# A two-block model on one core: the overflow branch behind expert 60, row-tiled sums for experts 60 to 63, and the last down matrix in another cut

## The chip, the core and the metric

The kernel runs on one core of a Trainium2 chip. The core's engines work side by side, each on its own queue of instructions: TensorE (PE) multiplies matrices, VectorE (DVE), ScalarE (ACT) and GpSimd (POOL) work on elements, and SyncE (SP) issues nearly all transfers. Sixteen DMA engines carry the transfers. The metric is the device time of one execution in microseconds (us); less is better.

## The reference, cut to what matters

The model maps 256 tokens of width 1024 through a short convolution block, an attention block, and a second block that ends in a mixture of 64 experts. Only the end of the second block is touched:

```python
def hier_moe(x, ...):            # 256 tokens; each goes to 2 of 64 experts
    ...
    def run_block(args):
        xb, e = args
        h = jax.nn.silu(xb @ w_gate[e]) * (xb @ w_up[e])   # 1024 -> 512
        return h @ w_down[e]                               # 512 -> 1024
    ...
    y = jnp.zeros((N, D)).at[slot_tok].add(ys * slot_gate[:, None])

h = h + hier_moe(rms_norm_2(h, norm2_gain), ...)
return rms_norm_2(h, final_gain)                           # the output
```

All matrices are in float32. One expert's gate, up and down matrix are 2 MB each, so the 64 experts are 384 MB that must come in from memory.

## The kernel before

Up to about 700 us of the span the kernel computes the first block and the mixer. From then on it goes through the experts in order, `for e in range(64)` (L1964). The experts are in groups of four (`q = e // 4`, `i = e % 4`). Each expert has room for 32 tokens (`CAP`), so a group fills the 128 columns or rows of TensorE.

**One expert.** `gateup(e)` (L1897) multiplies the gathered tokens with gate and up: eight steps of contraction, and in each of them four products that stand in four groups of 32 columns of TensorE and run at once. ACT and DVE form silu(gate) times up. `hidden(e)` (L1915) transposes the result on TensorE and copies it (DVE). `down(e)` (L1925) multiplies with the down matrix: four steps of contraction (`j`), and in each four products of 256 columns (`m`), again in four column groups at once. Four ACT copies (L1940) put the 32 rows of this expert into its place of `st["Y", q]`. At the end of a group `combine(q)` (L1942) multiplies the four experts' rows with the gates of the group, `st["C", q]` (made by `dtrans(q)`, L1880: one POOL product, two transposes, one ACT copy), and adds them up in four PSUM banks, `self.acc`, over all groups.

**Loads.** `moe_load` (L1654) issues the matrices from SP in the order of `ORDER` (number m = 3 e + 0, 1 or 2 for gate, up and down; at the end 189, 190, 188, 191, which is gate 63, up 63, down 62, down 63). SP reuses eight semaphores in turn, and before it issues a load it waits until the load of the same semaphore has landed: eight loads are under way at any time. `done(m)` (L1957) says how far the loads may be issued; SP is some four experts ahead of TensorE. Every matrix but the last is cut by rows, so that each of the 128 partitions reads one piece of 8 or 16 KB. The last one (m = 191, L1664 to L1669) is cut by columns: two loads of 512 columns, four pieces of 2 KB for each partition.

**The branch.** `overflow()` (L1809) handles tokens beyond the 32 of an expert. With these inputs it isn't taken. All engines read the count (L1812), compare and jump over it (L1813). On SP the other arm of this `If` waits on each of the eight load semaphores in turn and adds to it what the loads of the skipped body would have added. The branch stands behind expert 52 (`OVERFLOW_AFTER`), where SP has issued the loads up to m = 168, gate 56; at expert 60 `done(182)` has let out all 192.

**The end.** `self.busy(n)` (L311) is n products of 128 columns whose result nobody reads. They stand ahead of expert 62 (`WARM1` = 8) and in the last two experts (`WARM2`). For expert 63 `last(hf)` (L2001) multiplies with one half of the columns, and `total(hf)` (L2015) sums that half for group 15, squares it (ACT, with the sum of squares) and, for the left half, multiplies with the final gain (DVE). So the left half is summed, squared and scaled before the right half is multiplied. Then the norm (DVE, POOL), the scaling with it (ACT for the left halves, DVE for the right ones) and four transfers out (L2041) end the program.

Of the kernel before, what the change touches and what calls it, by code (L numbers as in the profile page):

```python
# [176 lines left out]
WARM, WARM1, WARM2, WARM4 = 12, 8, (14, 5, 0, 3), 11  # L177
# [19 lines left out]
OVERFLOW_AFTER = 52  # L197


class Build:  # L200
# [1453 lines left out]
    def moe_load(self, n):  # L1654

        a = self.a
        while self.npart < min(n, 192):
# [4 lines left out]
            if g == 2 and e == 63:  # L1664
                w = a["w_down_2"][0, e].rearrange("(k p) n -> p k n", p=128)
                self.wt[m] = []
                for j, t in enumerate(places):
                    t = t.rearrange("p (k n) -> p k n", k=4)
                    self.dma_in_order(t, w[:, :, 512 * j:512 * j + 512])  # L1669
                    self.wt[m].append(t)  # L1670
                continue
# [26 lines left out]
    def moe(self, out):  # L1698
# [191 lines left out]

        def cols(w, j, e):

            if e == 63:
                return w[:, 256 * j:256 * j + 256]
            return w.rearrange("q (p j k) -> q j p k", j=2, k=2)[:, j]
# [19 lines left out]
        def hidden(e, tile="rb3"):  # L1915

            b = self.bank()
            for k in range(2):
                x = st["h", e][:, k:k + 255:2] if e < 63 else st["h", e][:, 128 * k:128 * k + 128]
# [5 lines left out]
        def down(e, hT=None):  # L1925
            q, i = divmod(e, 4)
            hT = hT or hidden(e)
            b2 = self.bank()
            for j in range(4):
                for m in range(4):  # L1930
                    mm(b2[32 * m:32 * m + 32, :256], lhsT=hT[j], rhs=self.wt[3 * e + 2][j][:, m * 256:m * 256 + 256],  # L1931
                       start=j == 0, stop=j == 3, skip_group_check=True, tile_position=(0, 32 * m))
# [9 lines left out]
        def combine(q, ms=range(4)):  # L1942
            for m in ms:
                for tt in range(2):
                    i = mm(self.acc[2 * tt + m // 2][:, (m % 2) * 256:(m % 2) * 256 + 256],  # L1945
                           lhsT=st["C", q][:, tt * 128:tt * 128 + 128], rhs=st["Y", q][m],
                           start=False, stop=q == 15, skip_group_check=True)
                    if q == 15:
                        self.tc.keep_in_program_order(i)
# [14 lines left out]
        for e in range(64):  # L1964
            q, i = divmod(e, 4)
            if e == 62:
                self.busy(WARM1)
# [15 lines left out]
            if i == 3 and q < 15:  # L1983
                combine(q)
                dtrans(q + 1)


        hT = hidden(62)
        if OVERFLOW_AFTER == 62:
            overflow()  # L1990
        self.busy(WARM2[0])
        gateup(63)
        hT2 = hidden(63, "rb")
        self.busy(WARM2[1])
        down(62, hT)
        hT = hT2
        self.busy(WARM2[2])
        fs = sm("fs", 4)
        fs = fs.rearrange("p (t c) -> p t c", t=2)

        def last(hf):  # L2001
            b2 = self.bank()
            for j in range(4):
                for m in (2 * hf, 2 * hf + 1):
                    i = mm(b2[32 * m:32 * m + 32, :256], lhsT=hT[j], rhs=self.wt[191][hf][:, j, m % 2 * 256:m % 2 * 256 + 256],  # L2005
                           start=j == 0, stop=j == 3, skip_group_check=True, tile_position=(0, 32 * m))
                    self.tc.keep_in_program_order(i)
            for m in (2 * hf, 2 * hf + 1):
                o = st["Y", 15][m][96:128]
                if m % 2 == 0:  # L2010
                    A.activation(o, b2[32 * m:32 * m + 32, :256], AF.Copy)  # L2011
                else:
                    V.tensor_copy(o, b2[32 * m:32 * m + 32, :256])

        def total(hf):  # L2015
            combine(15, (2 * hf, 2 * hf + 1))
            for tt in range(2):
                scr = self.xp.tile([128, 512], BF16, name="yl", bufs=2)
                A.activation(scr, self.acc[2 * tt + hf], AF.Square, accum_out=fs[:, tt, hf:hf + 1])  # L2019
                if hf == 0:  # L2020
                    V.tensor_tensor(out=xt[tt][:, :512], in0=self.acc[2 * tt], in1=fg[:, :512], op=ALU.mult)

# [79 lines left out]
```

## Time and profile before

| | us |
|---|---|
| median of 3 runs | 1665.9 (1664.17 to 1668.14) |
| the profiled execution: its own time | 1667.51 |
| the profiled execution: span from first to last instruction | 1665.7 |
| of the span: TensorE busy | 1354.8 (81%) |
| DVE, ACT, POOL busy | 581.4, 498.4, 85.7 |
| bytes moved by DMA | 520.92 MB, mean 313 GB/s |

The times of a row are counted from the first instruction of the span. A busy TensorE is not one at its peak, since matmuls overlap; a float32 product shows as two instructions. Where two engines are busy together, only the one that the next step waits for counts, so the profile is read stage by stage, and from the end back.

### The profile page before, as it was taken

What the parts mean: (1) busy time and instruction counts of PE and PEld (TensorE: products, weight loads), DVE (VectorE), ACT (ScalarE), POOL (GpSimd) and SP (SyncE); (2) the same over time, 40 slices, a digit from 0 to 9 for tenths busy, and PEclk for the clock granted to TensorE, in tenths of its full rate; (3) what the DMA queues carried; (4) which work ended last, traced back from release to release, by engine and by line L of the source; (5) the groups of instructions that cost most, each with busy time, mean ns of one, the idle gap of its engine ahead of it and who ended that gap; (6) DMA issues with size and microseconds to landing.
All of it is one profiled execution on the core that took longest, in us unless ns stands there. A gap on an engine that the chain in (4) does not pass through costs nothing. (4 is left out here: it accounts for less than half of the span.)

```text
span 1665.7 us, 29509 instructions
## 1 busy us (share of the span) xinstructions
PE 1354.8 (81%) x12874; PEld 1063.8 (64%) x12874; DVE 581.4 (35%) x1043; ACT 498.4 (30%) x940; POOL 85.7 (5%) x121
## 2 busy tenths in 40 slices
PE   8999999999999989998867766666765776766666
PEld 8999999999999988885534433433433443333334
DVE  5777565877655567751100000000000000000001
ACT  4454444646444455631111110111111111111112
POOL 2000000210000051120000000000000000000000
PEclk9999999999999999999989889888888889888889
DMA  8555545443645544399999999999999999998996
GB/s 286 203 182 190 191 159 185 152 151 120 209 153 200 178 144 148 129 381 409 426 428 428 425 428 429 426 427 429 426 427 430 426 427 428 427 426 344 425 429 277
DMA packets 130917, 520.92 MB, mean 313 GB/s; under 512 B 6816, under 2 KB 84128, under 8 KB 96864
## 3 DMA queue, kind: packets, MB, share of 16 engines
q1 hardware_dynamic: 130496, 518.46, 78.0%
q8 instruction: 103, 1.69, 0.4%
q10 hardware_dynamic: 288, 0.52, 0.1%
q14 instruction: 30, 0.25, 0.0%
HBM read 517.91 MB, written 1.05 MB: 312 GB/s over the span
## 5 line engine op out<-in xcount | busy, mean ns | idle before, releaser
L1906 PE MATMUL bank<-gu,x 128*32 128x256 f32 x2400 | 265.4, 468 | 149.6 <-DMA gu<-in_w_up 97.8
L265 DVE TENSOR_TENSOR wl<-slot,wh 128x1024 fp32r<-128x1024 f32 (+1 forms) x210 | 256.3, 1222 | 125.7 <-ACT wh L264 124.8
L264 ACT ACTIVATE wh<-slot 128x1024 fp32r<-128x1024 f32 (+1 forms) x213 | 223.4, 1052 | 231.5 <-PE bank L274 149.6
L1906 PEld LDWEIGHTS bank<-gu,x 128*32 128x32 f32 x2400 | 114.8, 129 | 259.8 <-DMA gu<-in_w_up 111.8
L1912 DVE TENSOR_TENSOR dg<-dg,bank 64x256 f32<-64x256 f32 x64 | 27.1, 423 | 687.0 <-ACT dg L1911 687.0
L274 PE MATMUL bank<-x,wh 128*128 128x256 f32 x864 | 245.1, 284 | 0.0
L273 PE MATMUL bank<-x,wh 128*128 128x256 f32 x864 | 244.7, 283 | 0.0
L275 PE MATMUL bank<-x,wl 128*128 128x256 f32 x864 | 244.6, 283 | 0.0
L1906 PE MATMUL bank<-slot,x 128*32 128x256 f32 x1456 | 175.9, 446 | 36.3 <-DMA slot<-in_w_up 30.5
L1911 ACT ACTIVATE dg<-bank 64x256 f32<-64x256 f32 x64 | 24.0, 375 | 499.1 <-PE bank L1906 499.1
L1940 ACT ACTIVATE x<-bank 32x256 f32<-32x256 f32 x252 | 94.3, 374 | 240.2 <-PE bank L1931 234.1
L275 PEld LDWEIGHTS bank<-x,wl 128*128 128x128 f32 x864 | 165.9, 192 | 0.0
L274 PEld LDWEIGHTS bank<-x,wh 128*128 128x128 f32 x864 | 165.8, 192 | 0.0
L273 PEld LDWEIGHTS bank<-x,wh 128*128 128x128 f32 x864 | 165.8, 192 | 0.0
L274 PE MATMUL acc<-yl,wh 128*128 128x256 f32 x480 | 136.3, 285 | 0.0
L275 PE MATMUL acc<-yh,wl 128*128 128x256 f32 x480 | 136.1, 285 | 0.0
L273 PE MATMUL acc<-yh,wh 128*128 128x256 f32 x480 | 135.0, 285 | 1.2 <-ACT yh L349 1.2
L1906 PEld LDWEIGHTS bank<-slot,x 128*32 128x32 f32 x1456 | 74.4, 122 | 89.9 <-DMA slot<-in_w_up 42.8
L1931 PE MATMUL bank<-gu,rb 128*32 128x256 f32 x1248 | 77.5, 389 | 22.5 <-DVE rb L1922 11.3
L273 PEld LDWEIGHTS acc<-yh,wh 128*128 128x128 f32 x480 | 91.1, 192 | 1.9 <-ACT yh L349 1.8
L274 PEld LDWEIGHTS acc<-yl,wh 128*128 128x128 f32 x480 | 92.1, 192 | 0.2
L275 PEld LDWEIGHTS acc<-yh,wl 128*128 128x128 f32 x480 | 92.1, 192 | 0.1
(408 smaller groups left out, 1799.2 us busy)
## 6 DMA issues: line engine op xcount, KB each, us to landing
gu<-in_w_down SPq DMA_DIRECT2D x39, 2048.0 KB, 26.8
gu<-in_w_gate SPq DMA_DIRECT2D x39, 2048.0 KB, 27.4
gu<-in_w_up SPq DMA_DIRECT2D x35, 2048.0 KB, 26.8
slot<-in_w_up SPq DMA_DIRECT2D x47, 1024.0 KB, 24.6
slot<-in_w_gate SPq DMA_DIRECT2D x44, 1024.0 KB, 25.1
slot<-in_w_down SPq DMA_DIRECT2D x42, 1024.0 KB, 27.0
slot<-in_conv_ffn_w SPq DMA_DIRECT2D x33, 1024.0 KB, 5.0
slot<-in_mla_ffn_w SPq DMA_DIRECT2D x33, 1024.0 KB, 5.0
```

The lines of the kernel that those rows point to most:

```text
L264: i = nc.scalar.activation(h, src, AF.Copy)
L265: j = (low or nc.vector).tensor_tensor(out=l, in0=src, in1=h.bitcast(F32), op=ALU.subtract)
L273: mm(out, lhsT=wh, rhs=xh, start=start, stop=False, skip_group_check=skip)
L274: mm(out, lhsT=wh, rhs=xl, start=False, stop=False, skip_group_check=skip)
L275: mm(out, lhsT=wl, rhs=xh, start=False, stop=stop, skip_group_check=skip)
L1906: mm(b[32 * j:32 * j + 32, 0:256], lhsT=X[k][:, 32 * i:32 * i + 32], rhs=cols(self.wt[3 * e + j // 2][k], j % 2, e), start=k == 0, stop=k ...
L1911: A.activation(s[64:128], b[0:64, 0:256], AF.Silu)
L1912: V.tensor_tensor(out=s[0:64], in0=s[64:128], in1=b[64:128, 0:256], op=ALU.mult)
L1931: mm(b2[32 * m:32 * m + 32, :256], lhsT=hT[j], rhs=self.wt[3 * e + 2][j][:, m * 256:m * 256 + 256], start=j == 0, stop=j == 3, skip_group_ ...
L1940: A.activation(o, s, AF.Copy)
```

## The change

- `OVERFLOW_AFTER` goes from 52 to 60. The branch itself stays as it is.
- The last down matrix is cut by rows as well, but in another order of rows than the others. Row 32 j + 4 i + k of the matrix goes to partition 16 i + j; the loads hold k = 0, 1 and k = 2, 3. So each partition reads one piece of 8 KB in each of the two loads, and the outermost dimension of the source, i, has 8 rows. The columns of gate and up of expert 63 are taken in the same order (`cols`), and `hidden(63)` needs no case of its own.
- Experts 60 to 63 have no common `combine(15)`. Their down products (`product`) have 512 columns: column groups 0 and 1 hold the two halves of the result, groups 2 and 3 hold them once more. One ACT copy takes all 128 rows over (`sums`), and four products, one in each row group of 32 rows (`tile_position=(32 * m, 0)`), add token half m // 2 and column half m % 2 into bank m.
- `dtrans_last` makes the gates for this: for each of the four experts the gate columns four times over (4 POOL products, 8 transposes, 4 ACT copies, behind `combine(14)`).
- All `busy` products from expert 62 on are gone.
- The end is: hidden of 62, gate and up of 63, hidden of 63, then the products of 62, the first half of the contraction of 63, the sums of 62, the second half of 63, and the sums of 63. All four banks are squared after that; three of the four quarters are multiplied with the gain by DVE and scaled by ACT, and the fourth is done by DVE in one operation.

```diff
--- before.py
+++ after.py
@@ -174,7 +174,7 @@
 
 
 RING = 7
-WARM, WARM1, WARM2, WARM4 = 12, 8, (14, 5, 0, 3), 11
+WARM, WARM4 = 12, 11
 
 
 
@@ -194,7 +194,7 @@
 
 LOW_CONV, LOW_MLA, LOW_MIXER = (2,), (("dkv", 192),), ("gg2",)
 CAP = 32
-OVERFLOW_AFTER = 52
+OVERFLOW_AFTER = 60
 
 
 class Build:
@@ -1654,7 +1654,6 @@
     def moe_load(self, n):
 
 
-
         a = self.a
         while self.npart < min(n, 192):
             m = ORDER[self.npart]
@@ -1662,12 +1661,12 @@
             e, g = divmod(m, 3)
             places, both = self.moe_places(m)
             if g == 2 and e == 63:
-                w = a["w_down_2"][0, e].rearrange("(k p) n -> p k n", p=128)
+
+                w = a["w_down_2"][0, e].rearrange("(j i k) n -> i j k n", i=8, k=4)
                 self.wt[m] = []
                 for j, t in enumerate(places):
-                    t = t.rearrange("p (k n) -> p k n", k=4)
-                    self.dma_in_order(t, w[:, :, 512 * j:512 * j + 512])
-                    self.wt[m].append(t)
+                    self.dma_in_order(t, w[:, :, 2 * j:2 * j + 2].rearrange("i j k n -> i j (k n)"))
+                    self.wt[m] += [t[:, 1024 * k:1024 * k + 1024] for k in range(2)]
                 continue
             k = 4 if g == 2 else 8
             w = a[("w_gate_2", "w_up_2", "w_down_2")[g]][0, e].rearrange("(p k) n -> p k n", k=k)
@@ -1888,10 +1887,25 @@
             A.activation(ct, b[:, :256], AF.Copy)
             st["C", q] = ct
 
+        def dtrans_last():
+
+            for i in range(4):
+                Dq = self.xp.tile([128, 2, 128], F32, name="yl", bufs=2)
+                GP.tensor_tensor(out=Dq.rearrange("p t (r c) -> p t r c", r=4),
+                                 in0=st["G", 15][:, :, i:i + 1, :].to_broadcast([128, 2, 4, 32]),
+                                 in1=gt[:, :, 60 + i:61 + i, None].to_broadcast([128, 2, 4, 32]), op=ALU.mult)
+                b = self.bank()
+                for tt in range(2):
+                    PE.transpose(b[:, tt * 128:tt * 128 + 128], Dq[:, tt], I)
+                if i % 2 == 0:
+                    ct = self.xtile(6 + i // 2)
+                A.activation(ct[i % 2], b[:, :256], AF.Copy)
+                st["C", 15, i] = ct[i % 2]
+
         def cols(w, j, e):
 
             if e == 63:
-                return w[:, 256 * j:256 * j + 256]
+                return w.rearrange("q (c i j k) -> q j i c k", i=8, j=2, k=2)[:, j]
             return w.rearrange("q (p j k) -> q j p k", j=2, k=2)[:, j]
 
         def gateup(e, ks=range(8)):
@@ -1916,20 +1930,31 @@
 
             b = self.bank()
             for k in range(2):
-                x = st["h", e][:, k:k + 255:2] if e < 63 else st["h", e][:, 128 * k:128 * k + 128]
+                x = st["h", e][:, k:k + 255:2]
                 PE.transpose(b[:, 64 * k:64 * k + 64], x, I[0:64, 0:64])
             hT = self.rp.tile([128, 256], F32, name=tile)[:, :128]
             V.tensor_copy(hT, b[:, 0:128])
             return [hT[:, 64 * (j % 2) + 32 * (j // 2):64 * (j % 2) + 32 * (j // 2) + 32] for j in range(4)]
 
-        def down(e, hT=None):
+        def product(e, hT, b2, js=range(4)):
+
+
+            w = 512 if e >= 60 else 256
+            for j in js:
+                for m in range(4):
+                    c = m % 2 if e >= 60 else m
+                    i = mm(b2[32 * m:32 * m + 32, :w], lhsT=hT[j], rhs=self.wt[3 * e + 2][j][:, c * w:c * w + w],
+                           start=j == 0, stop=j == 3, skip_group_check=True, tile_position=(0, 32 * m))
+                    if e >= 62:
+                        self.tc.keep_in_program_order(i)
+
+        def down(e):
             q, i = divmod(e, 4)
-            hT = hT or hidden(e)
+            hT = hidden(e)
             b2 = self.bank()
-            for j in range(4):
-                for m in range(4):
-                    mm(b2[32 * m:32 * m + 32, :256], lhsT=hT[j], rhs=self.wt[3 * e + 2][j][:, m * 256:m * 256 + 256],
-                       start=j == 0, stop=j == 3, skip_group_check=True, tile_position=(0, 32 * m))
+            product(e, hT, b2)
+            if q == 15:
+                return sums(e, b2)
             if i == 0:
                 st["Y", q] = []
                 for m in range(2):
@@ -1939,14 +1964,24 @@
                 o, s = Y[m][32 * i:32 * i + 32], b2[32 * m:32 * m + 32, :256]
                 A.activation(o, s, AF.Copy)
 
-        def combine(q, ms=range(4)):
-            for m in ms:
+        def combine(q):
+            for m in range(4):
                 for tt in range(2):
-                    i = mm(self.acc[2 * tt + m // 2][:, (m % 2) * 256:(m % 2) * 256 + 256],
-                           lhsT=st["C", q][:, tt * 128:tt * 128 + 128], rhs=st["Y", q][m],
-                           start=False, stop=q == 15, skip_group_check=True)
-                    if q == 15:
-                        self.tc.keep_in_program_order(i)
+                    mm(self.acc[2 * tt + m // 2][:, (m % 2) * 256:(m % 2) * 256 + 256],
+                       lhsT=st["C", q][:, tt * 128:tt * 128 + 128], rhs=st["Y", q][m],
+                       start=False, stop=False, skip_group_check=True)
+
+        def sums(e, b2):
+
+            y = self.xp.tile([128, 512], F32, name=f"x{2 + e % 2}", bufs=1)
+            A.activation(y, b2, AF.Copy)
+            C = st["C", 15, e - 60]
+            for m in range(4):
+                p, tt = slice(32 * m, 32 * m + 32), m // 2
+                i = mm(self.acc[m], lhsT=C[p, tt * 128:tt * 128 + 128], rhs=y[p], start=False, stop=e == 63, skip_group_check=True,
+                       tile_position=(32 * m, 0))
+                if e >= 62:
+                    self.tc.keep_in_program_order(i)
 
         gather(0, (0,))
         gateup(0, range(4))
@@ -1963,8 +1998,6 @@
 
         for e in range(64):
             q, i = divmod(e, 4)
-            if e == 62:
-                self.busy(WARM1)
             gateup(e, range(8) if e else range(4, 8))
             if e == 20:
                 fg = self.wp.tile([128, 1024], F32, name="wl")
@@ -1982,49 +2015,31 @@
                 dtrans(0)
             if i == 3 and q < 15:
                 combine(q)
-                dtrans(q + 1)
-        hT = hidden(62)
-        if OVERFLOW_AFTER == 62:
-            overflow()
-        self.busy(WARM2[0])
+                if q < 14:
+                    dtrans(q + 1)
+                else:
+                    dtrans_last()
+
+
+        h62 = hidden(62)
         gateup(63)
-        hT2 = hidden(63, "rb")
-        self.busy(WARM2[1])
-        down(62, hT)
-        hT = hT2
-        self.busy(WARM2[2])
+        h63 = hidden(63, "rb")
+        b62, b63 = self.bank(), self.bank()
+        product(62, h62, b62)
+        product(63, h63, b63, (0, 1))
+        sums(62, b62)
+        product(63, h63, b63, (2, 3))
+        sums(63, b63)
         fs = sm("fs", 4)
         fs = fs.rearrange("p (t c) -> p t c", t=2)
-
-        def last(hf):
-            b2 = self.bank()
-            for j in range(4):
-                for m in (2 * hf, 2 * hf + 1):
-                    i = mm(b2[32 * m:32 * m + 32, :256], lhsT=hT[j], rhs=self.wt[191][hf][:, j, m % 2 * 256:m % 2 * 256 + 256],
-                           start=j == 0, stop=j == 3, skip_group_check=True, tile_position=(0, 32 * m))
-                    self.tc.keep_in_program_order(i)
-            for m in (2 * hf, 2 * hf + 1):
-                o = st["Y", 15][m][96:128]
-                if m % 2 == 0:
-                    A.activation(o, b2[32 * m:32 * m + 32, :256], AF.Copy)
-                else:
-                    V.tensor_copy(o, b2[32 * m:32 * m + 32, :256])
-
-        def total(hf):
-            combine(15, (2 * hf, 2 * hf + 1))
-            for tt in range(2):
+        for tt in range(2):
+            for hf in range(2):
                 scr = self.xp.tile([128, 512], BF16, name="yl", bufs=2)
                 A.activation(scr, self.acc[2 * tt + hf], AF.Square, accum_out=fs[:, tt, hf:hf + 1])
-                if hf == 0:
-                    V.tensor_tensor(out=xt[tt][:, :512], in0=self.acc[2 * tt], in1=fg[:, :512], op=ALU.mult)
-
-        last(0)
-        total(0)
-        self.busy(WARM2[3])
-        last(1)
-        total(1)
+            for hf in (1, 0):
+                if (tt, hf) != (1, 1):
+                    V.tensor_tensor(out=xt[tt][:, 512 * hf:512 * hf + 512], in0=self.acc[2 * tt + hf], in1=fg[:, 512 * hf:512 * hf + 512],
+                                    op=ALU.mult)
         f2 = sm("fs2", 2)
         r = []
         for tt in range(2):
@@ -2034,7 +2049,7 @@
             for tt in range(2):
                 for hf in range(2):
                     c = slice(hf * 512, hf * 512 + 512)
-                    if hf == 0:
+                    if (tt, hf) != (1, 1):
                         A.activation(xt[tt][:, c], xt[tt][:, c], AF.Copy, scale=r[tt])
                     else:
                         V.scalar_tensor_tensor(xt[tt][:, c], self.acc[2 * tt + 1], r[tt], fg[:, c], op0=ALU.mult, op1=ALU.mult)
```

## Rows read from the trace of the kernel before

**Rows 1.** Page, part 2: GB/s in 40 slices of 41.6 us.

```profile
GB/s 286 203 182 190 191 159 185 152 151 120 209 153 200 178 144 148 129 381 409 426 428 428 425 428 429 426 427 429 426 427 430 426 427 428 427 426 344 425 429 277
```

**Rows 2.** Chain of waits, 1645 us on: start us, us, what.

```profile
1621.15 27.02 DMA slot<-in_w_down
1648.31 1.94 PE bank L2005 x16
...
1650.69 1.99 PE acc L1945 x8
...
1657.34 0.39 ACT yl L2019
```

**Rows 3.** SP's own waits from 1400 us: us in total, times, longest.

```profile
SPq L1813 <- SPq L1813: 29.3, 5, 14.8
```

**Rows 4.** Instructions of L1813: ns min/median/max, first to last start.

```profile
L1813 SPq EVENT_SEMAPHORE  x8: 17/17/17, 1518.8 to 1533.5; - x8
...
L1813 PEldq COMPARE_BRANCH  x1: 6306/6306/6306, 1485.4 to 1485.4; - x1
```

**Rows 5.** Windows: us, busy of five engines, PE clock, DMA share, GB/s.

```profile
1524.00:1528.00 4.00, 4.00 (x48) 1.89 (x44) 0.00 (x0) 0.00 (x0) 0.00 (x0) 0.59 0.52 219
...
1532.00:1534.00 2.00, 2.00 (x21) 0.88 (x14) 0.00 (x0) 1.07 (x3) 0.00 (x0) 1.00 0.06 16
...
1540.00:1550.00 10.00, 7.30 (x94) 3.70 (x96) 0.71 (x2) 0.38 (x1) 0.00 (x0) 0.83 1.00 428
```

**Rows 6.** Loads issued at 1503.1, 1534.0, 1608.9, 1616.2, 1626.1: last number us to landing.

```profile
slot<-in_w_gate SPq DMA_DIRECT2D x1, 1024.0 KB, 30.2
gu<-in_w_up SPq DMA_DIRECT2D x1, 2048.0 KB, 7.4
gu<-in_w_up SPq DMA_DIRECT2D x1, 1024.0 KB, 31.9
slot<-in_w_down SPq DMA_DIRECT2D x1, 1024.0 KB, 29.4
h<-in_w_down SPq DMA_DIRECT2D x1, 1024.0 KB, 24.6
```

**Rows 7.** Timeline of the last experts: start us, us, engine, line, [idle before].

```profile
1616.28 0.64 PE L1906 MATMUL bank<-gu,x 128*32 128x256 f32 x2 [6.61 <-DMA gu<-in_w_up]
...
1623.35 1.93 PE L1931 MATMUL bank<-gu,rb 128*32 128x256 f32 x32 [0.38 <-DVE rb L1922]
...
1639.45 3.66 PE L1906 MATMUL bank<-gu,x 128*32 128x256 f32 x64
1643.17 0.38 ACT L1911 ACTIVATE dg<-bank 64x256 f32<-64x256 f32 x1 [7.93 <-PE bank L1906]
...
1644.43 0.29 DVE L1922 COPY rb<-bank 128x128 f32<-128x128 f32 x1 [0.42 <-PE bank L1920]
...
1653.07 1.29 DVE L2021 TENSOR_TENSOR wl<-acc,wl 128x512 f32<-128x512 f32 x2 [1.98 <-ACT yl L2019]
```

**Rows 8.** The same timeline after the last sums.

```profile
1657.34 0.60 ACT L2019 ACTIVATE yl<-acc 128x512 bf16<-128x512 f32 x1 [1.71 <-PE acc L1945]
...
1657.92 0.59 ACT L2019 ACTIVATE yl<-acc 128x512 bf16<-128x512 f32 x1
...
1658.48 1.14 POOL L361 TENSOR_TENSOR r2t<-ms,few 128x1 f32<-128x1 f32 x2 [172.97 <-DVE ms L359]
...
1659.09 1.33 ACT L2038 ACTIVATE wl<-wl,r2t 128x512 f32<-128x512 f32 x2 [0.49 <-POOL r2t L361]
...
1659.91 1.01 SPq L2041 DMA_DIRECT2D out<-wl  x2
```

**Rows 9.** TensorE at 1541 us, [idle before].

```profile
1541.40 0.64 PE L1906 MATMUL bank<-gu,x 128*32 128x256 f32 x2 [3.43 <-DMA gu<-in_w_up]
```

**Rows 10.** Windows, columns as in rows 5.

```profile
1616.00:1619.50 3.50, 3.22 (x32) 1.53 (x36) 0.00 (x0) 0.00 (x0) 0.00 (x0) 0.51 1.03 440
1626.00:1631.00 5.00, 1.85 (x19) 1.23 (x17) 0.00 (x0) 0.86 (x3) 0.00 (x0) 1.00 1.00 419
```


## The prediction

> **What bounds the kernel now.** I read the page's slices first: from about 790 us on the transfers run at 425 to 430 GB/s in nearly every slice [rows 1], so the loads set the time of the expert stage, and TensorE waits for them. Two slices differ. The last one (277) is the end, where compute is what is left. Slice 37, 1499 to 1541 us, has 344 against 426: 82/426 of 41.6 us, 8.0 us of full stream are missing. SP's own waits name the place: 29.3 us at L1813, the branch [rows 3]. SP does eight semaphore waits there, the last at 1533.5 us [rows 4], and the last load issued before the branch lands at 1503.1 + 30.2 = 1533.3 [rows 6]: SP lets the queue run empty before it issues again. The windows show how it ran empty: at 1524 to 1528 us the engines were busy to 0.52 and moved 219 GB/s, at 1532 to 1534 to 0.06, and at 1540 it is 428 again [rows 5]. So half of the sixteen had run out well before the other half.
>
> At the end the chain of waits goes from the first load of the last matrix, landed at 1648.2, over two rounds of product, copy and sum to the first square of the last half at 1657.34 [rows 2], and on over norm and scaling to the output transfers [rows 8]. The second load of that matrix lands at 1626.1 + 24.6 = 1650.7 [rows 6], before the second round starts.
>
> **The branch behind expert 60.** At expert 60 every load has been issued, so SP drains its queue with nothing behind it but the output, which it issues only near 1660 [rows 8]. What the drain cost is bounded from two sides. By landings: the next load is issued at 1534.0 and lands 7.4 later, at 1541.4 [rows 6], 8.1 after the one before; 2.097 MB at 428 GB/s [rows 5] take 4.9, so 3.2 us are lost. By bytes it is the 8.0 us above. The difference is that half of the engines that ran out early: a load has landed when its last engine is done, so the late half sets the landings, and it lost 3.2. The early half lost twice the excess more, 2 x (8.0 - 3.2) = 9.6 us; without the drain it keeps that lead. I take 3.2, since the last loads but two use all engines. Then the second half of up 63 lands at 1608.9 + 31.9 - 3.2 = 1637.6 and the second half of down 62 at 1616.2 + 29.4 - 3.2 = 1642.4 [rows 6].
>
> TensorE's jump over the body took 6.3 us [rows 4]. It moves to behind the sums of expert 60, some 1609 us, and gate-up 61 queues behind it; ACT, DVE and POOL have nothing late behind their short reads. Gate-up 61 before sat idle 6.6 us until up 61 landed at 1616.3 [rows 7], now 1613.1; with the jump it starts near 1616, 3 us late. From that start to the end of down 61 took 1623.35 + 1.93 - 1616.28 = 9.0 us [rows 7], with the longer down and the sums some 12.5; up 62 lands near 1627.7 and up 63 after 1635, so this is taken up there. Cost nothing; without those waits it would be 3 us. The same idle time covers the work of `dtrans_last` (six more transposes, three more POOL products) and the longer down of 60.
>
> **The last experts on TensorE.** Four contraction steps of 256 columns take 1.93 us in four column groups [rows 7] and 1.94 in two [rows 2]: 0.43 a step and 0.2 at the end, whatever the number of groups. A step of 512 columns is then 0.86. Hidden 63 is no bound: half a gate-up (3.66 / 2, [rows 7]) after 1637.6, and the 1.6 us from the end of gate-up to the copied transposes (1643.1 to 1644.7, [rows 7]) give 1641.0. From the landing at 1642.4 TensorE has: two steps of 62 (1.7), two of 63 (1.7), the sums of 62 (1.2), two steps of 63 with their end (1.9), the copy (0.6 for 512 columns, [rows 8], and 0.1), the sums of 63 (1.25): 8.45. The squares start at 1650.9 instead of 1657.34: 6.4 earlier.
>
> The sums of row groups don't occur in this trace. If four groups run at once, as column groups do, they cost one step and its end, 1.1; one after the other 4 x 0.86 + 0.25 = 3.7. The nearest row is that of the column groups, so I take 1.2; the sums stand in the chain twice, so the other end adds 5.0. [...]
>
> **The tail.** Two squares more: each starts 0.58 after the one before (1657.34, 1657.92, [rows 8]), 1.2 us. The DVE products with the gain wait for ACT's square of the same bank, 0.65 each [rows 7]; three now lie between squares and norm. In the order of the text they run from 1.3 to 3.25 us after the first square, and POOL starts at 3.6 instead of 1.14 (1658.48, [rows 8]): 2.5 later. ACT scales three quarters instead of two, 0.65 more [rows 8]. So the tail grows by 3.1 in that order, and by 1.2 + 0.65 = 1.8 if the norm's small operations are put ahead of the products. I take 2.6.
>
> **No busy products.** They cost nothing where TensorE waits anyway, but they kept the clock. [...] Now TensorE ends gate-up 62 near 1632 and has two transposes until 1635. If the clock falls there, half of gate-up 63 takes 3.6 instead of 1.8, of which 0.7 lie in the wait for the second half: 1.1 late. A fall in the last steps, where TensorE always has work, is less likely, and costs up to 3. I take half of the first, 0.6.
>
> **Sum.** -6.4 + 2.6 + 0.6 = -3.2 us. The profiled execution took 1667.51 us (span 1665.7, 1.8 around it), so 1664.3 for one like it; it stands 1.6 above the median of 1665.9, from which the forecast is 1662.7. This is as much as 0.2% (3.3 us), about what a measurement of this kernel can tell from no change. Own range: 1660.5 (tail 1.8, clock held, a little more on landings) to 1665.
>
> **The last matrix, and the rivals.** In this sum the last matrix is never late. On sixteen engines its second half lands at 1650.7 - 3.2 = 1647.5, and TensorE comes to it at 1642.4 + 1.7 + 1.7 + 1.2 = 1647.0: half a us. On eight engines each half takes 1.049 MB / 219 GB/s = 4.8 us (rate from [rows 5]); if these are the eight with 9.6 us of lead, both are in by 1642.4.
>
> *Eight engines without a lead (0.18).* If the load goes on eight engines and these are the late ones, the halves start at 1642.4 and land at 1647.2 and 1652.0. TensorE then waits 5.0 us, and every us beyond 1647.0 is paid in full: -3.2 + 5.0 = +1.8, 1667.7; with the clock fallen in that wait 1.5 to 3 more, up to 1670.7. For it: half of the engines are late by the time of the branch [rows 5], and nothing in the trace names which. Against it: no load of this trace is seen on fewer than all. [...]
>
> *Row groups one after the other (0.07).* -3.2 + 5.0 = +1.8, 1667.7. For it: the sums before were one after the other, 1.99 for four [rows 2]. Against it: the four write four banks and use four sets of rows.
>
> *The branch still in front of loads (0.05).* If the order of SP's queue leaves loads behind the branch, the drain costs its 3.2 again: 1665.9. Against it: the text lets all out before.
>
> **Chances.** Forecast 0.70, of which 0.37 faster by over 0.2% and 0.33 within. Eight late engines 0.18: 0.10 within, 0.08 slower. Row groups 0.07: 0.04 and 0.03. Branch 0.05, within. So faster 0.37, same 0.52, slower 0.11. The range 1660.2 to 1668.4 takes in the forecast's own and most of the rivals.
>
> **What will show it.** In the profile after: slice 37 at 425 or more and a wait of SP at the branch after its last load; the second half of down 62 landing near 1642 and TensorE's first step after it at once; the two halves of the last matrix either before 1645 (lead), near 1647 (sixteen) or at 1647 and 1652 (late eight); sums of about 1.2 us; the first square near 1651.5; the POOL operation 2.5 to 3.6 us behind it; the granted clock from 1632 on. The prediction is wrong if the landings move by much else than 3.2, if the last load lands after 1648, or if the sums take over 2 us.

## The result: the loads ahead of the last matrix came late, not only the matrix

The changed kernel takes 1674.2 us (median of 10 executions, 1670.9 to 1682.0) where the kernel before takes 1666.2 (10 executions beside it, 1664.2 to 1669.3). The ratio is 1.0051, with a 95% interval of 1.0037 to 1.0065: slower by about half a per cent. The forecast was 1662.7, with a range of 1660.2 to 1668.4. The runs further down were measured beside other executions of the kernel before (medians of 1666.5 to 1667.4), so they are compared by their ratios. The profiled execution of the changed kernel took 1671.6 us, its span is 1669.8.

The hole at the branch is gone. These are the page's slices of the changed kernel in GB/s (40 slices of 41.7 us): slice 37 holds 427, where [rows 1] have 344. The price stands in the last slice, 125 instead of 277.

```profile
GB/s 307 181 195 204 162 187 157 175 150 127 178 174 205 168 167 109 154 390 419 426 427 428 427 426 429 429 426 431 425 428 427 428 428 428 427 427 427 428 423 125
```

The windows of the changed kernel at the end (us, busy time of PE, PEld, DVE, ACT and POOL with counts, granted clock, DMA share, GB/s):

```profile
1620.00:1625.00 5.00, 3.49 (x34) 0.90 (x26) 0.00 (x0) 0.60 (x1) 0.00 (x0) 1.00 1.01 418
1625.00:1630.00 5.00, 4.47 (x65) 2.02 (x62) 0.08 (x1) 0.38 (x1) 0.00 (x0) 1.00 0.93 320
1630.00:1635.00 5.00, 1.18 (x10) 0.62 (x14) 0.64 (x2) 0.00 (x0) 0.00 (x0) 0.87 0.91 197
1635.00:1640.00 5.00, 4.05 (x40) 1.55 (x40) 0.00 (x0) 0.00 (x0) 0.00 (x0) 0.50 0.90 185
1640.00:1645.00 5.00, 4.07 (x34) 1.50 (x30) 0.72 (x2) 0.38 (x1) 0.00 (x0) 0.50 0.82 221
1645.00:1650.00 5.00, 4.50 (x32) 0.80 (x24) 0.00 (x0) 0.42 (x1) 0.00 (x0) 0.76 0.25 88
1650.00:1655.00 5.00, 2.79 (x24) 0.81 (x24) 0.00 (x0) 0.18 (x1) 0.00 (x0) 1.00 0.13 54
```

The last two columns belong together. In [rows 5] a busy share of 0.52 moved 219 GB/s and 1.00 moved 428. Here 0.90 moves 185: the engines are busy, but a packet takes twice as long. Worked out for 1635 to 1640: 16 engines x 5 us x 0.90 are 72 us of engine time, and 185 GB/s x 5 us are 113 packets of 8 KB, 0.64 us for each; at 1.00 and 428 it is 0.31. The single packets of 8 KB in the trace say the same: 0.31 us up to 1628, 0.61 on average from 1630 to 1641 (half of them between 0.55 and 0.64), 0.31 again for nearly all after 1646. In the last row two engines are left, at full rate (2 x 26.7 = 53 GB/s).

A load is complete once for each engine that carries it (sixteen completions in the trace for the usual cut; eight for the new one, which by itself, in cut52 below, keeps 0.50 of the sixteen engines busy), and it has landed with the last of them: the product that waits for the first new load starts at 1652.21, behind the last completion at 1652.1. The loads ahead of the last matrix are late as well. The last column here is the time from issue to landing, for the loads issued at 1601.8 (second half of up 63) and 1609.1 (second half of down 62):

```profile
gu<-in_w_up SPq DMA_DIRECT2D x1, 1024.0 KB, 37.6
slot<-in_w_down SPq DMA_DIRECT2D x1, 1024.0 KB, 38.4
```

They land at 1639.4 and 1647.5. TensorE's timeline shows who waits (start us, us, engine, line, tiles, [idle before]):

```profile
1634.84 3.64 PE L1920 MATMUL bank<-gu,x 128*32 128x256 f32 x32 [3.42 <-SPq L1812]
1639.43 3.63 PE L1920 MATMUL bank<-gu,x 128*32 128x256 f32 x28 [0.95 <-SPq L1812]
1643.99 0.50 PE L1934 MATMUL bank<-cst,dg 64*128 64x64 f32 x2 [0.94 <-DVE dg L1926]
1644.42 5.08 PE L1946 MATMUL bank<-slot,rb 128*32 128x512 f32 x32
1652.21 1.92 PE L1946 MATMUL bank<-slot,rb 128*32 128x512 f32 x16 [2.71 <-SPq L1812]
1654.07 1.14 PE L1981 MATMUL acc<-x,x 32*128 32x512 f32 x8
1656.98 1.92 PE L1946 MATMUL bank<-h,rb 128*32 128x512 f32 x16 [1.77 <-SPq L1812]
```

SP's L1812 is named as releaser, but SP's waits there were behind its last load; what the products really wait for are the landings of up 63 (1634.8, 1639.4) and of the two halves of the last matrix, whose last completions come at 1652.1 and 1656.9. The first square, in the chain of waits, comes at 1660.90 instead of 1657.34 [rows 2]:

```profile
1659.68 1.22 PE acc L1981 x8
1660.90 0.12 ACT yl L2038
```

Up to the load of gate 62 the two traces tell the opposite story: it landed at 1618.9, 7.1 us ahead of the kernel before. Some 3.0 to 3.4 of that were there ahead of expert 52 already (single executions differ by as much before the change plays any part); the rest, 3.8 to 4.1, is the drain that is gone. The lead is lost in the last six transfers ahead of the last matrix: 6.6, 5.7, 3.6, 1.4, -0.3 and -1.8 us are left at up 62, gate 63, the two halves of up 63 and the two of down 62.

### The profile page after: what moved, and what is told of

Same layout as the page of the kernel before. It is cut to its first block, busy times and chain, and to the rows that moved or that the text cites. A ratio compares the mean times of both kernels' runs of the same rounds, so it can differ in the third digit from the quotient of the medians.

```text
span 1669.8 us, 29430 instructions
## 1 busy us (share of the span) xinstructions
PE 1354.3 (81%) x12836; PEld 1052.8 (63%) x12836; DVE 582.7 (35%) x1041; ACT 497.3 (30%) x934; POOL 84.8 (5%) x124
## 5 line engine op out<-in xcount | busy, mean ns | idle before, releaser
L1965 ACT ACTIVATE x<-bank 32x256 f32<-32x256 f32 x240 | 90.0, 375 | 226.6 <-PE bank L1946 223.9
L1946 PE MATMUL bank<-gu,rb 128*32 128x256 f32 (+1 forms) x1248 | 80.2, 399 | 24.3 <-DVE rb L1936 11.7
## 6 DMA issues: line engine op xcount, KB each, us to landing
gu<-in_w_up SPq DMA_DIRECT2D x35, 2048.0 KB, 26.8
```

The source lines that it names most:

```text
L1946: i = mm(b2[32 * m:32 * m + 32, :w], lhsT=hT[j], rhs=self.wt[3 * e + 2][j][:, c * w:c * w + w], start=j == 0, stop=j == 3, skip_group_chec ...
L1965: A.activation(o, s, AF.Copy)
```

## The experiments

**Theory and rivals.** The theory after the two traces: the sixteen engines are not level (at the same place in the queue) when the last matrix begins: the completions of one load lie 11.7 us apart from first to last at 1609. So the engines that are ahead start on the last matrix while the others still fill earlier loads. With the new cut the two hinder each other: either by where they write, or by what they read. The rivals: eight engines only have twice the bytes; a queue that is never emptied stretches its last loads by itself; the new end or the missing busy products are the loss.

A first group takes the change apart.

**nat60: the change without the new cut.**

```diff
-                w = a["w_down_2"][0, e].rearrange("(j i k) n -> i j k n", i=8, k=4)
+                w = a["w_down_2"][0, e].rearrange("(p k) n -> p k n", k=4)
...
-                    self.dma_in_order(t, w[:, :, 2 * j:2 * j + 2].rearrange("i j k n -> i j (k n)"))
+                    self.dma_in_order(t.rearrange("p (k n) -> p k n", k=2), w[:, 2 * j:2 * j + 2])
...
-            if e == 63:
-                return w.rearrange("q (c i j k) -> q j i c k", i=8, j=2, k=2)[:, j]
```

> The changed kernel, but the last down matrix cut like all others (row 4p + k on partition p, 128 outermost rows, two transfers of 1 MB). If the cut into eight outermost rows is the cause: all loads stay 7.1 us ahead of before up to the last one, up 63 lands near 1633.7, down 62 near 1638.6 and the last matrix by 1644; 8.5 us of TensorE after 1638.6 give the first square near 1647 to 1649 and, with a tail longer by 0.5, a time of 1659 to 1661, 5 to 7 below before (of which 4.1 from the branch, about 3 from the end). If the late half of the DMA engines or the missing busy products are the cause, the last five loads stretch here too (down 62 near 1647) and the time stays at 1670 to 1674.

1661.5 us; ratio to before 0.9966 (0.9954 to 0.9978). Against the changed kernel's 1.0051 (1.0036 in again60, below) that is 12 to 14 us, all from how one matrix is cut (the columns of gate and up 63 only follow that order). TensorE's timeline and two windows of nat60:

```profile
1634.84 2.00 PE L1918 MATMUL bank<-gu,x 128*32 128x256 f32 x28 [0.47 <-SPq L1812]
1637.78 0.45 PE L1932 MATMUL bank<-cst,dg 64*128 64x64 f32 x2 [0.94 <-DVE dg L1924]
1638.15 3.64 PE L1944 MATMUL bank<-slot,rb 128*32 128x512 f32 x32
1642.34 1.92 PE L1944 MATMUL bank<-slot,rb 128*32 128x512 f32 x16 [0.55 <-SPq L1812]
1644.19 1.14 PE L1979 MATMUL acc<-x,x 32*128 32x512 f32 x8
1645.27 1.92 PE L1944 MATMUL bank<-h,rb 128*32 128x512 f32 x16
1647.97 1.14 PE L1979 MATMUL acc<-x,x 32*128 32x512 f32 x8 [0.78 <-ACT x L1975]
...
1630.00:1635.00 5.00, 3.21 (x43) 1.54 (x46) 0.71 (x2) 0.38 (x1) 0.00 (x0) 1.00 0.95 392
1635.00:1640.00 5.00, 4.06 (x50) 1.65 (x46) 0.71 (x2) 0.38 (x1) 0.00 (x0) 1.00 0.55 228
```

From the landing of down 62 (1639.8) on, the end runs nearly without a gap. 0.55 of the engines' time moves 228 GB/s: each packet has its usual time (0.32 us, worked out as above), although here, too, the completions of one load lie 11.4 us apart. Engines that are not level do no harm with the usual cut. This kernel is faster than both others.

**old60: the branch alone.**

```diff
-OVERFLOW_AFTER = 52
+OVERFLOW_AFTER = 60
```

> The kernel before with nothing changed but the branch, behind expert 60 instead of 52. If the branch costs by landings what the two traces show (the loads were 3.0 us apart before it and 7.1 after it), 4.1 us less: 1662. By the prediction's 3.2: 1663. If a queue that is never emptied stretches the last loads by itself (the rival to the cut), or if the jump of 6.3 us at expert 60 is paid, 1666 to 1670.

1663.4 us; 0.9969 (0.9957 to 0.9982). The landings go from 0.6 to 1.5 us ahead, at the loads before the branch, to 4.7 ahead: 3.2 to 4.1 us gained. The last four loads are still 4.0 ahead, so a queue that is never emptied stretches its last loads by 0.7 us at most.

**nat52: the new end alone** (nat60 with `OVERFLOW_AFTER = 52`).

> The changed kernel with the branch back behind expert 52 and the last matrix cut like the others: the new end alone (row-tiled sums, no busy products, new tail). Landings as before: down 62 at 1645.7. By the prediction's chain of 8.45 us the first square comes at 1654.2 instead of 1657.3, the tail is longer by 0.5 as measured: -2.7, 1663.5; with the clock fallen in gate-up 63, up to 1665. If the new end is the loss, 1668 or more.

1664.7 us; 0.9988 (0.9977 to 0.9999): some 2 us gained, just clear of the noise. The new end is no loss.

**cut52: the new cut with level engines** (the changed kernel with `OVERFLOW_AFTER = 52`; the completions of one load lie 2 us apart).

> The changed kernel with the branch back behind expert 52, so that all sixteen DMA engines are level when the last matrix begins, near 1645.7. If eight engines only share its bytes (4.8 us for each half), the halves land at 1650.5 and 1655.3, the first square comes near 1659 and the time is 1668 to 1670. If the packets of this cut hinder each other, as the doubled time per packet in the changed kernel says (90% busy at 190 GB/s), each half takes up to 9.7 us: 1655.4 and 1665, and 1676 to 1680. If only the late half of the engines is the matter, nothing is late here: 1664 to 1665.

1669.9 us; 1.0018 (1.0008 to 1.0028); 5 us over nat52. The halves landed at 1649.7 and 1654.6, 4.8 us apart: this is the rival of eight engines that share the bytes, at their full rate. Behind the branch at 52 the cut costs 5 us, behind the branch at 60 it costs 12 to 14; the prices are not independent. Timeline and windows:

```profile
1644.64 1.92 PE L1946 MATMUL bank<-slot,rb 128*32 128x512 f32 x16 [0.82 <-DMA slot<-in_w_down]
1649.84 1.92 PE L1946 MATMUL bank<-slot,rb 128*32 128x512 f32 x16 [3.28 <-DMA slot<-in_w_down]
1651.70 1.14 PE L1981 MATMUL acc<-x,x 32*128 32x512 f32 x8
1654.60 1.93 PE L1946 MATMUL bank<-h,rb 128*32 128x512 f32 x16 [1.76 <-DMA h<-in_w_down]
...
1638.00:1640.00 2.00, 1.54 (x30) 1.09 (x28) 0.00 (x0) 0.00 (x0) 0.00 (x0) 1.00 1.03 430
1642.00:1644.00 2.00, 1.82 (x16) 0.31 (x15) 0.29 (x1) 0.00 (x0) 0.00 (x0) 1.00 0.73 180
1646.00:1650.00 4.00, 0.72 (x12) 0.19 (x8) 0.00 (x0) 0.60 (x1) 0.00 (x0) 1.00 0.50 193
```

In the 2 us in which the last usual load and the first new one overlap, 0.73 of the engines' time moves 180 GB/s (246 at full share): the slow packets show here too, but briefly. The second half of down 62 came 1.2 us late by it. Later, with eight engines busy, the rate comes near the usual one (193 at 0.50).

A second group keeps the branch at 60 and separates the number of engines, what they read and where they write.

**near60: other reads, same eight rows, same partitions.**

```diff
-                w = a["w_down_2"][0, e].rearrange("(j i k) n -> i j k n", i=8, k=4)
+                w = a["w_down_2"][0].rearrange("e r n -> (e r) n")[30720:31264]
+                w = w.rearrange("(i u k) n -> i u k n", i=8, k=4)[:, :16]
```

> The changed kernel; the two last transfers keep eight outermost rows and their partitions, but read 16 pieces of 8 KB that lie 16 KB apart for each row, instead of 128 KB apart (they read rows of the down matrices of experts 60 and 61, so expert 63's product has the wrong numbers; the work is the same). If what the packets read slows them (the distance of 128 KB), their time falls back to 0.31 us here, eight engines only share the bytes, the halves land by 1645 and 1650 and the time is 1664 to 1667. If it is where they write (an engine writes partitions that another engine is still filling with an earlier load), nothing changes against the changed kernel: 190 GB/s at 90% busy from 1630 to 1640, halves near 1652 and 1657, 1672 to 1676.

1676.1 us; 1.0062 (1.0040 to 1.0083). Reading nearby pieces helps nothing:

```profile
1630.00:1635.00 5.00, 2.15 (x24) 0.81 (x16) 0.71 (x2) 0.38 (x1) 0.00 (x0) 1.00 0.90 193
1635.00:1640.00 5.00, 3.04 (x32) 1.35 (x32) 0.00 (x0) 0.00 (x0) 0.00 (x0) 0.58 0.89 200
```

**far60: reads 128 KB apart, usual partitions.** nat60 with

```diff
-                w = a["w_down_2"][0, e].rearrange("(p k) n -> p k n", k=4)
+                w = a["w_down_2"][0].rearrange("e r n -> (e r) n")[0:4096]
+                w = w.rearrange("(p k) n -> p k n", k=32)
```

> The kernel with the last matrix cut like all others (nat60, 1661.5), but the two last transfers read pieces of 8 KB that lie 128 KB apart, from the first eight experts' down matrices (so expert 63's product has the wrong numbers). [...] If the distance of 128 KB is the cause: the last loads stretch, over 1666. If it is where the packets write: as nat60, 1660 to 1663.

1662.7 us; 0.9970 (0.9957 to 0.9984), as nat60. Reads 128 KB apart harm nothing:

```profile
1630.00:1635.00 5.00, 3.28 (x42) 1.38 (x38) 0.71 (x2) 0.38 (x1) 0.00 (x0) 1.00 0.89 367
1635.00:1640.00 5.00, 3.97 (x46) 1.63 (x46) 0.71 (x2) 0.38 (x1) 0.00 (x0) 1.00 0.54 224
```

**i16_60: sixteen outermost rows.**

```diff
-                w = a["w_down_2"][0, e].rearrange("(j i k) n -> i j k n", i=8, k=4)
+                w = a["w_down_2"][0, e].rearrange("(j i k) n -> i j k n", i=16, k=4)
...
-                return w.rearrange("q (c i j k) -> q j i c k", i=8, j=2, k=2)[:, j]
+                return w.rearrange("q (c i j k) -> q j i c k", i=16, j=2, k=2)[:, j]
```

> The changed kernel with sixteen outermost rows instead of eight in the last two transfers (row 64 j + 4 i + k on partition 8 i + j; the columns of gate and up follow). If too few engines were all, this is nat60: 1660 to 1663. If the packets hinder each other by where they write, and the sixteen rows go to engines in their order, so that an engine writes other partitions than with the usual cut, packets of over 0.31 us show again between 1630 and 1645 and the time is 1664 to 1672. If by what they read (here 256 KB apart), the same slow stretch, so that this run tells the number of engines from the other two, and far60 and near60 tell those two apart.

1667.1 us; 1.0005 (0.9993 to 1.0018). All sixteen engines are busy from 1630 to 1635 (a share of 1.00), and the stretch is still there, though shorter: some 6 us over nat60.

```profile
1630.00:1635.00 5.00, 1.28 (x10) 0.66 (x14) 0.39 (x2) 0.00 (x0) 0.00 (x0) 0.97 1.00 234
1635.00:1640.00 5.00, 5.00 (x60) 2.54 (x52) 0.00 (x0) 0.00 (x0) 0.00 (x0) 0.69 0.70 238
```

The first row has the slow packets without any idle engine: 234 GB/s at 1.00.

**chunk60: same reads, other partitions.**

```diff
-                w = a["w_down_2"][0, e].rearrange("(j i k) n -> i j k n", i=8, k=4)
+                w = a["w_down_2"][0, e].rearrange("(c b i k) n -> c i b k n", c=4, b=4, k=4)
...
-                    self.dma_in_order(t, w[:, :, 2 * j:2 * j + 2].rearrange("i j k n -> i j (k n)"))
+                    for c in range(4):
+                        self.dma_in_order(t[32 * c:32 * c + 32], w[c, :, :, 2 * j:2 * j + 2].rearrange("i b k n -> i b (k n)"))
```

> The changed kernel, each of the last two transfers in four of 256 KB that fill 32 partitions each: the eight engines read the same pieces in the same order as in the changed kernel, but row i goes to partitions 4 i to 4 i + 3 of each 32 instead of to 16 i to 16 i + 15 (the contraction of expert 63 then meets its rows in another order than gate and up, so its numbers are wrong; the work is the same). If what is read is the cause: no change, 1672 to 1676, packets doubled. If where it is written: another time, below 1670 if fewer engines meet on the same partitions. Six more transfers in SP's queue wait for earlier landings, the last one for down 62; this can cost up to 2 by itself.

1666.9 us; 1.0002 (0.9991 to 1.0014): 6 to 8 us less than the changed kernel for the same pieces in the same order, put elsewhere. The place is not the only difference: SP issued the eight transfers between 1616.1 and 1643.7, the changed kernel its two at 1614.0 and 1619.0. The later ones overlap less with the loads ahead of them, and a part of the 6 to 8 us can come from that.

```profile
1630.00:1635.00 5.00, 3.65 (x53) 2.07 (x48) 0.71 (x2) 0.38 (x1) 0.00 (x0) 1.00 0.93 324
1635.00:1640.00 5.00, 2.69 (x31) 0.99 (x26) 0.00 (x0) 0.00 (x0) 0.00 (x0) 0.79 0.79 192
```

The first two of the eight (partitions 0 to 63) were issued in time, at 1616.1 and 1621.0, and they show the place by itself. The first was complete on six engines at 1630.6 to 1633.4, the second 1.2 to 1.8 us later on each, while the other engines still filled earlier loads; four packets of 0.31 us are 1.24. The windows from 1630 to 1632, of chunk60 and then of the changed kernel, are worked out as above to 0.31 and 0.69 us:

```profile
1630.00:1632.00 2.00, 1.06 (x19) 0.36 (x11) 0.42 (x1) 0.38 (x1) 0.00 (x0) 1.00 0.89 373
1630.00:1632.00 2.00, 1.02 (x6) 0.46 (x6) 0.64 (x2) 0.00 (x0) 0.00 (x0) 1.00 0.93 176
```

From 1635 to 1638, when the early engines are at the transfers to partitions 64 to 127, the packets of chunk60 take 0.6 us as well.

The four agree on one cause. Reads changed, partitions kept: no change (near60, 193 GB/s at 0.90). Usual partitions, far reads: no slow packet (far60, 367 at 0.89). Same reads, other partitions: no slow packet in the first two transfers (chunk60, 373 at 0.89). Sixteen rows in another order of partitions, with no engine idle: slow packets again (i16_60, 234 at 1.00). What slows the packets in these runs is where they write, while other engines write too.

**again60 and busy60: the clock.** again60 is the changed kernel once more, beside busy60, which puts three groups of busy products back.

```diff
+WARM, WARM1, WARM2, WARM4 = 12, 8, (14, 5), 11
...
+            if e == 62:
+                self.busy(WARM1)
             gateup(e, range(8) if e else range(4, 8))
...
         h62 = hidden(62)
+        self.busy(WARM2[0])
         gateup(63)
         h63 = hidden(63, "rb")
+        self.busy(WARM2[1])
```

> The changed kernel once more, as the measure for the next run on the same chip: 1672 to 1676, the last loads stretched as before (190 to 200 GB/s at 90% busy between 1630 and 1640).

> The changed kernel with busy products put back at three of their old places (8 ahead of gate-up 62, 14 ahead of gate-up 63, 5 behind hidden 63). If the clock's lower level that the changed kernel shows from 1635 to about 1647 is part of the loss, up to 3 less: 1671. If the landings of the last loads set the end, as the transfers' theory has it, the clock is covered: the same as the changed kernel within 1, though the granted clock may stay at 1.00.

again60: 1672.3 us, 1.0036 (1.0018 to 1.0053). busy60: 1673.3 us, 1.0038 (1.0024 to 1.0053). In busy60 the clock stays up to 1660, and nothing is gained by it:

```profile
1635.00:1640.00 5.00, 4.08 (x34) 3.41 (x33) 0.29 (x1) 0.00 (x0) 0.00 (x0) 1.00 0.89 210
1640.00:1645.00 5.00, 2.16 (x32) 1.43 (x32) 0.00 (x0) 0.00 (x0) 0.00 (x0) 1.00 0.92 215
```

The granted clock is 1.00 where the changed kernel has 0.50; the transfers are as slow (210 GB/s at 0.89). The last half of the last matrix lands 37.9 us behind gate 62, in the changed kernel 38.0 (34.8 in again60, where the clock is down too), and TensorE waits 1.77 us ahead of the last products in both. So the clock that falls in the changed kernel up to 1647 is a consequence of the waits (0.50 where they stand empty, 1.00 in busy60 where products fill them), and covered by them.

The two medians alone would not show that, since busy60 pays for the clock at another place:

```profile
1660.42 3.41 PE L1946 MATMUL bank<-h,rb 128*32 128x512 f32 x16 [1.77 <-SPq L1812]
```

In its profiled execution the clock falls behind that last wait (0.50 from 1662 to 1664), and the last products of expert 63 take 3.41 us instead of 1.92. There nothing covers it: 1.5 us. How many of its other executions pay this is not known.

## Why the prediction was wrong, and where it was right

**The step that failed** is the landing of the loads ahead of the last matrix. The sum, and with it the rival of the late eight, carried "the second half of down 62 at 1642.4" as settled, and let the eight engines delay only the last matrix itself, 4.8 us for each half. The size of that delay was right (4.8 in cut52), but the packets also slowed the engines that still filled earlier loads: up 63 came at 1639.4 instead of 1637.6 and down 62 at 1647.5 instead of 1642.4, in an execution that ran some 3 us ahead of the one before. With the usual cut the same load came at 1639.8 (nat60, 1.9 to 2.9 us ahead before the branch), where the step has it. The rate behind the 4.8, 219 GB/s [rows 5], was read where the other half of the engines had run dry; nothing in the trace before showed half of them on one cut while the others were still on another.

**Lead or late half.** The forecast had all eight engines in the early half, the rival all eight in the late one. Six were early and two late, as far as completions show it: six of the eight completions of the first new load came between 1634.9 and 1642.8, the last two at 1651.1 and 1652.1, and from 1650 to 1655 two engines were left. So neither case was the real one, and the two late ones alone set the landing. The rival (1667.7, to 1670.7 with the clock fallen) had the halves 4.8 us apart, as measured (1652.1, 1656.9), but 5 us too early, since it began from the same 1642.4.

That the new loads could go on eight engines was the condition of two of the cases, and no row before showed it: the experts' loads all have sixteen completions there. The runs show it as to the number: both new loads have eight completions, and in cut52 they share the bytes at half of the full rate (193 GB/s at a share of 0.50). Which eight engines they are, no run shows. What the sum lacked is the price of a packet that is written among those of another cut. One engine moves 26.8 GB/s here (428 GB/s over sixteen engines), a packet of 8 KB in 0.31 us. With the usual cut it keeps that time although the completions of one load lie 11.4 us apart (nat60); with the new one it takes 0.61 on average from 1630 to 1641, twice as long. far60, near60, i16_60 and chunk60 show that it depends on the partitions written. What two engines share there, and which partitions each of them writes, no run shows.

**The branch.** Right. Predicted 3.2 by landings, with 8.0 by bytes as the other end; measured 3.8 to 4.1 between the two traces, 3.2 to 4.1 in old60, 4 to 5 in its time. Slice 37 is at 427, and SP's waits at the branch are 36.4 us in all, behind its last load (SP's own waits from 1400 us on: us in total, times, longest):

```profile
SPq L1812 <- SPq L1812: 36.4, 6, 14.3
```

TensorE's jump (6.3 us again) cost nothing, as predicted: gate-up 61 started at 1610.25, 1.1 us after up 61 had landed, and TensorE still waited 1.5 us for up 62 at 1624.4.

**The last experts.** Right. Two steps of 512 columns take 1.92 us (1.9 reckoned), four 3.64, the sums in row groups 1.14 (1.2 taken against 3.7), and on sixteen engines the wait for the last matrix is 0.55 us (half a us reckoned). The rival of serial row groups is out. The changes between column and row groups, for which the sum has no term, are small: with 0.86 us a step, the sums of nat60 start 0.13 us behind their turn (1644.19 after two steps from 1642.34), and the next step starts 1.08 us after them, 0.2 more than a step.

**The tail** was mis-sized: predicted 2.6 (1.8 to 3.1), measured 0.6. From the first square to the end of the span it is 8.9 us (1669.8 - 1660.9) where before it was 8.4 (1665.7 - 1657.34). Executions differ here: old60, with the old end, has 7.8 (1661.1 - 1653.35), against which it is 1.2. DVE took the norm's first small operation after two of the three products:

```profile
1661.62 1.29 DVE L2041 TENSOR_TENSOR wl<-acc,wl 128x512 f32<-128x512 f32 x2 [16.80 <-ACT yl L2038]
1662.83 0.15 DVE L2046 TENSOR_TENSOR fs<-fs 128x1 f32<-128x1 f32 x1
...
1663.24 0.58 POOL L361 TENSOR_TENSOR r2t<-ms,few 128x1 f32<-128x1 f32 x1 [73.81 <-DVE ms L359]
1663.86 1.33 ACT L2053 ACTIVATE wl<-wl,r2t 128x512 f32<-128x512 f32 x2 [0.53 <-POOL r2t L361]
...
DMA to landing us min/median/max: 2.1/2.2/2.7
```

POOL starts 2.3 us behind the first square, not 3.6, and ACT scales 1.2 us later than before ([rows 8], 1.75 behind the square; here 2.96). The last output is issued 1.7 us later than before (4.9 behind the first square, 3.2 before), near the low end of the prediction. The rest was not in the sum: the four outputs now go out over 1.2 us instead of 0.7, and land after 2.1 to 2.7 us each, where the kernel before needed 3.0 to 3.8 (old60 2.6 to 3.3).

**The clock** was expected to cost 0.6, half the price of a slow half of gate-up 63 (3.6 us instead of 1.8; a granted clock of 0.51 stands in [rows 10]). The runs show such a half, 3.63 us at 0.50 in the changed kernel (1639.43) against 2.00 at 1.00 in nat60 (1634.84), but no run shows the 0.6: in nat60 the clock held 1.00 through gate-up 63, and in the changed kernel, where it fell, the wait for the last matrix covered it.

**The sum without the last matrix** would have been -3.2; nat60 has -5.7 (0.34%). What it is better by is mostly the tail (1.4 to 2.0) and the clock (0.6). Beside the 1665.9 that the forecast started from, its ratio gives 1660.2, a little under the forecast's own range of 1660.5 to 1665. So for a kernel in which the last matrix is cut as the others are, the direction and the terms of the branch and of the last experts were right, and the whole gain was sized at little over half. The case nearest to what came was given 0.18, and priced at 5 us where 12 to 14 were paid.

## What to carry to other kernels

A transfer that is cut unlike its neighbours is costed together with the loads still in flight ahead of it: look for the DMA share and GB/s side by side, since a share near 1 with half the rate (0.90 and 185 GB/s here) means packets that take longer, not engines without work (0.50 and 193 in cut52). Before an odd cut goes to the end of a long stream, ask whether the engines are level there; a drain that looks like a loss may be what keeps them level (the completions of one load lay 2 us apart at the end behind the drain at 1533, 11.7 at 1609 without it). So the prices of two parts of a change need not add up: here the cut cost 5 us with the drain behind expert 52, moving the drain gained about 4, and without the drain at 52 the cut cost 12 to 14. The cut with the 128 partitions outermost was the one that stood a lag of 11 us (nat60, 392 GB/s at 0.95).

## What the runs showed of the hardware

- In the kernel before, the sixteen DMA engines drift apart in a saturated stream (428 GB/s at a share of 1.00): the completions of one load lay 0.5 us apart at 640 us and 10.3 us apart by 1500, half of the engines within 4 us and the other half behind; after the drain at 1533 it was 0.5 us again, and 2 us at the end. What sets the late ones back was not tried.
- Packets of 8 KB that took 0.31 us took around 0.6 while engines with another cut wrote among them (185 GB/s at a share of 0.90). In near60 (193 at 0.90), i16_60 (234 at 1.00) and chunk60 (192 at 0.79) slow packets show in the same stretch, in nat60 (392 at 0.95) and far60 (367 at 0.89) none.
- In cut52 the eight engines, alone from 1646 on, soon ran near their usual packet time: 193 GB/s at a share of 0.50, by which a packet of 8 KB takes 0.34 us.
- Four transfers of 256 KB out of the core landed in 2.1 to 2.7 us when issued over 1.2 us (changed kernel), and in 3.0 to 3.8 and 2.6 to 3.3 when issued over 0.7 (before, old60).
